# RWKV stage of a streaming-encoder layer: small products padded with zeros to the whole TensorE array

## The chip, the cores and the metric

One of the eight NeuronCores of a Trainium2 chip runs the whole kernel. A core has TensorE (PE: products of a stationary operand, loaded first, with a moving one), VectorE (DVE), ScalarE (ACT), GpSimd (POOL) and SyncE (SP, which issues the transfers here). The metric is the device time of one execution in microseconds (us).

## The reference

One layer mixes 4,096 tokens of width 1,024 in four head groups of width 256 and adds a gated embedding, a residual and a layer norm. The change touches the RWKV-7 group only: four heads of width 64, each with a 64x64 state that is updated token by token.

```python
def step(state, inp):
    w_t, r_t, k_t, v_t, kk_t, ab_t = inp
    sa = jnp.einsum('bhvk,bhk->bhv', state, -kk_t)
    state = (state * w_t[:, :, None, :] + sa[..., None] * ab_t[:, :, None, :]
             + v_t[..., None] * k_t[:, :, None, :])
    return state, jnp.einsum('bhvk,bhk->bhv', state, r_t)
```

The inputs of the step (receptance r, key k, value v, the decay w from a low-rank product, the removal key kk, the rate a) come from one projection of the tokens with a shift by one token. Behind the recurrence stand a norm by heads, a bonus term and a gate.

## The kernel before

The kernel runs pooling, retention, mLSTM, RWKV and the output stage one after another. The RWKV stage (`_rwkv_out`) takes the tokens in 16 blocks of 256, a block as four chunks of 64 (cc = 0, 1 picks a pair of chunks, e = 0, 1 the chunk in it), and solves the recurrence of a chunk in matrix form: products of decayed keys and queries (scores `gp`, kept in `g1`), the inverse `X` of a triangular 64x64 matrix per chunk and head (eight chunk pairs and heads side by side on the free axis), and a state `S` that is carried from chunk to chunk. The two chunks of a pair lie in the two halves of the 128 partitions; heads are counted by p and hh, with head hh in one half of the partitions where keys stand there.

All float32 products take two instructions each on TensorE; the dense projections (`la`, `k`, `r`, `v`, `g`) are exact splits into a high and a low part, three products each.

A block passes through pieces: the projections `la`, `k`, `r`, `v` and the gate `g`; `l` (low-rank decay and rate), `n` (norm of the removal key), `m` (elementwise keys and queries `BK`, `AR`), `bn` (bonus), `s0`, `s1` (transposed keys `ST`), `p0`, `p1` (scores), `vt` (transposed values into `SAV`), `inv` and `iv` (the diagonal blocks of 16 of the inverse: the matrix goes through DRAM to a layout with 64 partitions, 22 VectorE operations work on it, and the result goes through DRAM to X), and `pt`, `px`, `pu`, `py` (32x32 products that join the blocks of 16 to 32 and 64). `chain` runs the four chunks one after another, in three steps each:

- step 1: `ry` = AR S + (scores) SAV, and its half `bs` is copied to `R`;
- step 2: `sa` = X R, copied into the other half of `SAV`;
- step 3: `ds` = ST SAV updates the state (`Se` on POOL, four operations on VectorE, L657 to L661), and a last group of `ry` products gives the output.

The string ORDER sets how the pieces of three neighbouring blocks are woven together; TensorE keeps this order (`keep_in_program_order`). In iteration i the pieces marked .0 run for block i, those marked .1 for block i - 1, and each C is one step of the chain of block i - 2. "v.0/2" means two of the eight contraction steps of v; a dense step of two column halves is six products. Each iteration begins with

```python
C la.0 C k.0/2 C k.0 C r.0/2 C l.0 r.0/3 C r.0/2 n.0 r.0/2 C vt.1 r.0 m.0 C g.0/4 ...
```

so the first C (step 1 of chunk 0) and `la` stand ahead of the second C (step 2, `sa`), and `inv`, `iv` of block i are the last pieces of iteration i. The order on the other engines and the semaphores are made by a scheduler, from the accesses to tiles and their parts and from priorities (`soon()` raises one).

Of the kernel before, what the change touches and what calls it, by code (L numbers as in the profile page):

```python
# [29 lines left out]
ORDER = "C la.0 C k.0/2 C k.0 C r.0/2 C l.0 r.0/3 C r.0/2 n.0 r.0/2 C vt.1 r.0 m.0 C g.0/4 C g.0 v.0/2 C s0.0 v.0/1 pt.1 C p0.0/1 v.0/1 px.1 C p0.0 v.0/2 bn.0 v.0 pu.1 s1.0 p1.0/1 py.1 p1.0 inv.0 iv.0"  # L30
# [12 lines left out]
class Trunk:  # L43
# [27 lines left out]
    def fetch(self, hi, lo, src, nm, eng):  # L71
        """load float32 data and split it exactly into hi + lo"""
# [14 lines left out]
    def weights(self, name, g0, w=G, pool=None, bufs=5, gates=False):  # L87
        """hi and lo parts of columns g0..g0+w of a weight matrix"""
# [4 lines left out]
        lo = pool.tile([P, KT, c], F32R, name=f"wl_{name}_{g0}", tag=f"wl{tag}", bufs=bufs)  # L93
        hi = pool.tile([P, KT, c], F32R, name=f"wh_{name}_{g0}", tag=f"wh{tag}", bufs=bufs)
# [54 lines left out]
    def dense_k(self, jobs):  # L149
        """the same in steps of one contraction tile, in this order on the engine"""  # L150
# [19 lines left out]
    def silu_gate(self, sg, z):  # L170
        """twice z * sigmoid(z)"""
# [13 lines left out]
    # ------------------------------------------------------------------ RWKV  # L185
# [6 lines left out]
    def _rwkv_out(self, es):  # L192
# [17 lines left out]
        wla = self.lazy("w_rw", 3 * G, P)  # L210
# [3 lines left out]
        lraw = p1.tile([P, 2, P], F32, name="lraw", tag="km")  # L214
# [29 lines left out]
        zero = p1.tile([P, 512], F32, name="rzero", tag="km")  # L244
        Q.memset(zero, 0.0)
        for i in range(2):
# [3 lines left out]
            for e in range(2):  # L250
                nc.sync.dma_start(out=XD[i][:, e].rearrange("j a c -> j (a c)"), in_=zero[0:64])
        state = {"n": 0}
# [4 lines left out]
        def mixed(b, out, z, c0, n):  # L257
            """z + (previous token's z - z) * mu, by columns"""
# [11 lines left out]
        # what a block goes through, in pieces: generators that yield the time of the products they have issued  # L270
# [53 lines left out]
        def l(b):  # L324
            # low-rank decay and rate
# [4 lines left out]
            for g in range(2):  # L330
# [8 lines left out]
            tw = p1.tile([P, 2, TB], F32, name=f"tw{b}", tag="tw")  # L339
# [18 lines left out]
        def n(b):  # L358
            # squared norm of the removal key, by tokens in the order of the rows of its products
            k = bl[b]["k"]  # L360
            sq = p1.tile([P, 2, TB], F32, name=f"sq{b}", tag="km")
# [3 lines left out]
            for cc in range(2):  # L365
                for e in range(2):
                    for p in range(2):
                        t0 = cc * P + 64 * e
                        mm(n2[64 * (1 - e):64 * (1 - e) + 64, cc, 2 * p:2 * p + 2], sq[:, p, t0:t0 + 64], ones2,
                           start=True, stop=True)  # L370
            # rows (kappa, beta) of an even chunk, (beta, kappa) of an odd one
# [4 lines left out]
            for e in range(2):  # L376
                sl = slice(64 * (1 - e), 64 * (1 - e) + 64)
                Q.tensor_copy(out=rc[sl, :, e], in_=ri[sl])
# [8 lines left out]
        def m(b):  # L387
            k, r, ta, E, Ei = (bl[b][x] for x in ("k", "r", "ta", "E", "Ei"))
            km = p1.tile([P, 2, TB], F32, name=f"km{b}", tag="km")
# [5 lines left out]
            BK = p1.tile([P, 2, 2, 4, 64], F32, name=f"BK{b}", tag="BK")  # L395
# [14 lines left out]
            rk = p1.tile([P, 2, TB], F32, name=f"rk{b}", tag="tw")  # L410
            Q.tensor_tensor(out=rk, in0=r, in1=km, op=ALU.mult)
            ST = [p4.tile([P, 2, 2, P], F32, name=f"ST{b}_{cc}", tag="ST") for cc in range(2)]
            g1 = [p4.tile([P, 2, 2, 2, P], F32, name=f"g1{b}_{cc}", tag="g1") for cc in range(2)]
# [5 lines left out]
        def bn(b):  # L419
            rk = bl[b]["rk"]  # L420
            bn = wk.tile([P, 2, 4], F32, name=f"bn{b}", tag="wk")
            for cc in range(2):
                for e in range(2):
                    for p in range(2):
                        t0 = cc * P + 64 * e
                        mm(bn[64 * e:64 * e + 64, cc, 2 * p:2 * p + 2], rk[:, p, t0:t0 + 64], rkw[:, p],
                           start=True, stop=True)
# [5 lines left out]
        def s_(b, cc):  # L433
            # token-major copies of (kappa, beta)
# [11 lines left out]
        def p_(b, cc):  # L446
            # scores of the chunk
            BK, rc, AR, g1 = (bl[b][x] for x in ("BK", "rc", "AR", "g1"))
            gp = [wk.tile([P, 2, 2, P], F32, name=f"gp{b}_{cc}_{hh}", tag="wk") for hh in range(2)]
            for hh in range(2):  # L450
                sl = slice(64 * hh, 64 * hh + 64)
                for p in range(2):
                    for e in range(2):
                        mm(gp[hh][:, p, e], BK[sl, p, cc, 2 * e:2 * e + 2].rearrange("p a t -> p (a t)"),
                           AR[cc][sl, p, 2 * e:2 * e + 2].rearrange("p a t -> p (a t)"), start=True, stop=True)
                for p in range(2):
                    for e in range(2):
                        i = 2 * p + hh
                        V.scalar_tensor_tensor(out=g1[cc][:, hh, p, e], in0=gp[hh][:, p, e],  # L459
                                               scalar=rc[:, cc, e, i:i + 1], in1=msk[:, 64 * e:64 * e + P],  # L460
                                               op0=ALU.mult, op1=ALU.mult)
                yield 0.87
# [10 lines left out]
        def vt(b):  # L473
            v = bl[b]["v"]
            SAV = [p4.tile([P, 2, G], F32, name=f"SAV{b}_{cc}", tag="SAV") for cc in range(2)]
# [48 lines left out]
        def iv(b):  # L524
# [3 lines left out]
            with self.soon():  # L528
                # the four blocks of 4 on the diagonal, row by row from below
# [7 lines left out]
                # pairs of blocks: X12 = X11 (N12 X22), the inner product where N has zeros  # L537
# [17 lines left out]
                X = p2.tile([P, 8, 64], F32, name=f"X{b}", tag="X")  # L555
# [1130 lines left out]
```

## Time and profile before

| what | value |
|---|---|
| three runs | 2904.56, 2904.88, 2898.69 us, median 2904.56 |
| span of the profiled execution | 2898.2 us |
| TensorE busy | 2773.1 us |
| VectorE, GpSimd, ScalarE busy | 2270.0, 1156.9, 974.5 us |

The profile is that of one execution; its span runs from the first to the last instruction. What lies around the span is not shown for it; the fastest run shown is 0.5 us above the span, the median 6.4. The RWKV stage's products run from about 1,250 to 2,160 us. A row of the timeline shows the start in us from the span's start, the duration, the engine, the line of kernel.py, what is written and read, and the shapes; "x8" is a run of eight like instructions, whose duration is that from the first's start to the last's end. Since products are pipelined, the cost of one is the distance between starts, not its own duration. All small products are recorded under line 273, the helper `mm`; the tile's name tells them apart. "64*64" is the part of the array that the stationary operand fills, rows * columns. PEclk is the granted clock of TensorE: 1.0 is 2.4 GHz, 0.5 is 1.2 GHz.

### The profile page before, as it was taken

The numbers are of one execution on the slowest core, as the hardware profiler recorded it, in microseconds if no ns is written. First come the engines' busy times: TensorE is split into PE (matmuls) and PEld (weight loads), VectorE is DVE, ScalarE is ACT, GpSimd is POOL, SyncE is SP. The second block draws the span as 40 slices with busy tenths as digits, with TensorE's granted clock in tenths as the row PEclk, the third lists the DMA queues.
The fourth block names the chain that finished last, engine by engine and source line by source line (L and its number), as shares of the span: only waits on it lengthen the run. The fifth ranks groups of instructions, "written<-read, shape, count | busy, mean of one in ns | idle before, by whom it ended". The sixth has DMA issues, their size and how long they took to land.

```text
span 2898.2 us, 57364 instructions
## 1 busy us (share of the span) xinstructions
PE 2773.1 (96%) x21940; PEld 2466.1 (85%) x21940; DVE 2270.0 (78%) x5639; ACT 974.5 (34%) x2100; POOL 1156.9 (40%) x1231
## 2 busy tenths in 40 slices
PE   7899999999999999798999999999999999999997
PEld 7898888878999999688999999998998788777885
DVE  5657788887999999976777777778847566689997
ACT  3423223234433333333333333334423233432221
POOL 6654555553333333421232333223326111156665
PEclk9899999999999999888999999999999999999998
DMA  7743222223211111321111111112437444643441
GB/s 241 218 142 102 59 66 66 63 72 110 71 59 56 59 53 55 103 59 29 47 34 41 44 37 45 34 45 60 133 106 260 149 139 138 221 153 139 148 157 66
DMA packets 250499, 281.13 MB, mean 97 GB/s; under 512 B 69488, under 2 KB 166512, under 8 KB 250224
## 3 DMA queue, kind: packets, MB, share of 16 engines
q1 hardware_dynamic: 250224, 277.46, 30.5%
q8 instruction: 172, 2.82, 0.4%
q14 instruction: 103, 0.84, 0.1%
HBM read 209.69 MB, written 67.70 MB: 96 GB/s over the span
## 4 chain that ended last, share of the span: by engine, by line
PE 41%; DVE 10%; POOL 3%; DMA 2%; issue 2%; ACT 1%; SPq 0%; POOLq 0%; DVEq 0%; ACTq 0%
PE ry L273 3%; PE gp L273 2%; DVE ro L1578 2%; DVE ro L1557 1%; PE sa L273 1%; PE l L273 1%; PE zg L154 1%; DVE ro L1560 1%; PE zpl L147 1%; PE zpl L145 1%; PE zpl L146 1%; PE zg L155 1%; PE zg L156 1%; POOL ro L1561 1%; PE zpe L145 1%
## 5 line engine op out<-in xcount | busy, mean ns | idle before, releaser
L1336 ACT CAST Ah<-xr 128x512 fp32r<-128x512 f32 x189 | 117.0, 620 | 277.7 <-PE zrb L1372 58.7
L1337 DVE TENSOR_TENSOR Al<-xr,Ah 128x512 fp32r<-128x512 f32 x135 | 99.8, 739 | 76.5 <-ACT Ah L1336 75.7
L677 POOL TENSOR_TENSOR SAV<-SAV,bon 64x256 f32<-64x256 f32 x64 | 40.7, 636 | 283.9 <-PE ry L273 282.3
L85 DVE TENSOR_TENSOR xl<-rawx,xh 128x512 fp32r<-128x512 f32 x148 | 120.9, 821 | 39.8 <-ACT xh L84 38.9
L145 PE MATMUL zqk<-xh,wh_w_ml 128*128 128x256 f32 x512 | 149.1, 291 | 1.1 <-ACT xh L1078 1.1
L146 PE MATMUL zqk<-xl,wh_w_ml 128*128 128x256 f32 x512 | 149.1, 291 | 0.3 <-DVE xl L1079 0.3
L147 PE MATMUL zqk<-xh,wl_w_ml 128*128 128x256 f32 x512 | 149.2, 291 | 0.0
L84 ACT CAST xh<-rawx 128x512 fp32r<-128x512 f32 x148 | 91.6, 619 | 168.8 <-DMA rawx<-in_xT 72.3
L1337 POOL TENSOR_TENSOR Al<-xr,Ah 128x512 fp32r<-128x512 f32 x54 | 71.8, 1330 | 135.7 <-ACT Ah L1336 72.2
L1561 POOL TENSOR_TENSOR ro<-ro,ln_b 128x512 f32<-128x512 f32 x64 | 100.6, 1591 | 53.9 <-DVE ro L1560 53.9
L660 DVE SCALAR_TENSOR_TENSOR S<-ds,eC,Se 64x64 f32<-64x64 f32 x256 | 72.5, 283 | 53.4 <-PE ds L273 48.7
L866 POOL TENSOR_TENSOR rot<-rot,sw 128x256 f32<-128x256 f32 x64 | 69.4, 1085 | 94.2 <-DVE sw L865 88.5
L145 PEld LDWEIGHTS zqk<-xh,wh_w_ml 128*128 128x128 f32 x512 | 98.0, 191 | 3.6 <-ACT xh L1078 1.6
L147 PEld LDWEIGHTS zqk<-xh,wl_w_ml 128*128 128x128 f32 x512 | 98.1, 192 | 2.4
L146 PEld LDWEIGHTS zqk<-xl,wh_w_ml 128*128 128x128 f32 x512 | 98.2, 192 | 2.0 <-DVE xl L1079 0.8
L459 DVE SCALAR_TENSOR_TENSOR g<-gp,rc,c_rmask 128x128 f32<-128x128 f32 x256 | 72.1, 343 | 33.9 <-PE gp L273 32.8
L145 PE MATMUL zu<-xh,wh_w_pl 128*128 128x256 f32 x256 | 78.7, 308 | 14.7 <-ACT xh L84 8.9
L1356 POOL TENSOR_TENSOR xr<-xr,xr 128x512 f32<-128x512 f32 x27 | 35.5, 1316 | 141.8 <-DVE xr L1353 141.7
L146 PE MATMUL zu<-xl,wh_w_pl 128*128 128x256 f32 x256 | 78.2, 305 | 12.0 <-DVE xl L85 12.0
L1185 DVE SCALAR_TENSOR_TENSOR xc<-zc,c_convw,xc 128x256 f32<-128x256 f32 x192 | 86.2, 497 | 0.4
L273 PE MATMUL ry<-SAV,g 64*64 64x64 f32 (+1 forms) x1024 | 83.5, 223 | 0.0
L798 DVE SCALAR_TENSOR_TENSOR dp<-s,c_pinv,us 64x256 f32<-64x256 f32 (+1 forms) x64 | 44.5, 695 | 47.9 <-POOL s L784 41.7
(1120 smaller groups left out, 10675.9 us busy)
## 6 DMA issues: line engine op xcount, KB each, us to landing
rawx<-in_xT SPq DMA_DIRECT2D x148, 256.0 KB, 3.3
xr<-in_xT SPq DMA_DIRECT2D x108, 256.0 KB, 2.9
mr<-in_xT SPq DMA_DIRECT2D x64, 256.0 KB, 3.1
rp<-in_x SPq DMA_DIRECT2D x64, 256.0 KB, 3.1
s<-rp SPq DMA_DIRECT2D x64, 256.0 KB, 2.5
yo<-y SPq DMA_DIRECT2D x16, 1024.0 KB, 4.9
ro<-s SPq DMA_DIRECT2D x16, 1024.0 KB, 5.0
out<-ro SPq DMA_DIRECT2D x32, 512.0 KB, 2.6
```

The source lines that it names most:

```text
L84: nc.scalar.copy(out=hi, in_=raw)
L85: eng.tensor_tensor(out=lo, in0=raw, in1=hi.bitcast(F32), op=ALU.subtract)
L145: nc.tensor.matmul(out, lh(k), rh(k), start=(k == 0 and (apart or i == 0)), stop=False, skip_group_check=True)
L146: nc.tensor.matmul(out, lh(k), rl(k), start=False, stop=False, skip_group_check=True)
L147: nc.tensor.matmul(out, ll(k), rh(k), start=False, stop=(k == nk - 1), skip_group_check=True)
L273: mm = lambda *args, **kw: keep(nc.tensor.matmul(*args, **kw))
L459: V.scalar_tensor_tensor(out=g1[cc][:, hh, p, e], in0=gp[hh][:, p, e], scalar=rc[:, cc, e, i:i + 1], in1=msk[:, 64 * e:64 * e + P], op0=AL ...
L660: V.scalar_tensor_tensor(out=Sn[hv, p, hv], in0=ds[hv, p], scalar=eC[hv, p, c:c + 1], in1=Se[hv, p], op0=ALU.mult, op1=ALU.add)
L1185: V.scalar_tensor_tensor(out=xc[:, t], in0=zc[t // 2][:, t % 2, j:j + TB], scalar=cw[:, t, j:j + 1], in1=xc[:, t], op0=ALU.mult, op1=ALU.add)
L1336: self.nc.scalar.copy(out=hi, in_=src)
L1337: eng.tensor_tensor(out=lo, in0=src, in1=hi.bitcast(F32), op=ALU.subtract)
L1561: Q.tensor_tensor(out=rg, in0=rg, in1=ln["ln_b", g], op=ALU.add)
```

## The change

- The products of `ry`, `sa`, `l`, `n` and `bn` take all 128 rows and columns of the array. The operands that were cut to a half are replaced by tiles that hold zeros in the other half (`LZ`, `SAVS`, `G1` with three groups of 64 of which the middle one is zero, `RR`), cleared once at the start, `SAV` in each block. `n` and `bn` use half as many products. Output rows that hold nothing of use are not read.
- The inverses of two blocks live in one tile `XX` with 18 positions of 64 columns, and `sa` takes two neighbouring positions, of which one is the chunk's own.
- `ds` is two products of 128 columns in place of four of 64. The state update is one VectorE addition `T` = ds + S and four ScalarE scalings by the chunk's decay; `Se` on POOL is gone.
- The score products alternate between the two heads hh; all of a pair of chunks are one piece.
- ORDER changes from the second step of chunk 2 on: `bn` stands behind `g`, `p0` and `p1` are whole, `s1` and the last `v` steps stand between the chain's last step and `pu`, and `p1` comes ahead of `py`.
- Room for it: BK, tw and km move to a weight buffer that `la`'s narrower weights leave free; `lraw`, the zeros for DRAM and a tile of the gated embedding use another tag.

```diff
-ORDER = "... C g.0/4 C g.0 v.0/2 C s0.0 v.0/1 pt.1 C p0.0/1 v.0/1 px.1 C p0.0 v.0/2 bn.0 v.0 pu.1 s1.0 p1.0/1 py.1 p1.0 inv.0 iv.0"
+ORDER = "... C g.0/4 C g.0 bn.0 v.0/2 C s0.0 v.0/1 pt.1 C p0.0 v.0/2 px.1 C v.0/1 s1.0 v.0/2 pu.1 v.0/1 p1.0 v.0 py.1 inv.0 iv.0"
...
+        LZ = [cp.tile([P, 2, P], F32R, name=f"LZ{g}", tag=f"LZ{g}") for g in range(2)]
...
+            Q.memset(LZ[g][other].bitcast(F32), 0.0)
+            A.copy(out=LZ[g][own], in_=lraw[own])
...
+        SAVS = [[cp.tile([P, 2, G], F32, ...) for cc in range(2)] for i in range(2)]
+        own_ = self.wp.tile([P, 2 * D], F32, name="own", tag="wlg")
+        BK_ = own_[:, 0:D].rearrange("p (a c g t) -> p a c g t", a=2, c=2, g=4)
+        tw_, km_ = (own_[:, o:o + H].rearrange("p (a t) -> p a t", a=2) for o in (D, D + H))
+        G1 = [[cp.tile([P, 2, 2, 2, 3, 64], F32, ...) for cc in range(2)] for i in range(2)]
+        XX = cp.tile([P, 18, 64], F32, name="XX", tag="XX")
+        RR = [cp.tile([P, 2, P], F32, name=f"RR{e}", tag=f"RR{e}") for e in range(2)]
+        for t in [t for x in SAVS + G1 for t in x] + RR + [XX]:
+            Q.memset(t, 0.0)
...
+            for g in range(2):
                 for p in range(2):
                     mm(lz[g][:, p], LW[g][:, p], lah[:, g], start=(p == 0), stop=False, skip_group_check=True)
-                    mm(lz[g][:, p], LW[g][own, p], lal[own], start=False, stop=True, skip_group_check=True)
+                for p in range(2):
+                    mm(lz[g][:, p], LZ[g][:, p], lal, start=False, stop=(p == 1), skip_group_check=True)
...
-                for e in range(2):
-                    for p in range(2):
-                        t0 = cc * P + 64 * e
-                        mm(n2[64 * (1 - e):64 * (1 - e) + 64, cc, 2 * p:2 * p + 2], sq[:, p, t0:t0 + 64], ones2, ...)
+                for p in range(2):
+                    mm(n2[:, cc, 2 * p:2 * p + 2], sq[:, p, cc * P:cc * P + P], ones2, start=True, stop=True)
...
-            for hh in range(2):
-                sl = slice(64 * hh, 64 * hh + 64)
-                for p in range(2):
-                    for e in range(2):
+            for p in range(2):
+                for e in range(2):
+                    for hh in range(2):
+                        sl = slice(64 * hh, 64 * hh + 64)
                         mm(gp[hh][:, p, e], BK[sl, p, cc, 2 * e:2 * e + 2]..., AR[cc][sl, p, 2 * e:2 * e + 2]..., ...)
...
+                    Q.memset(SAV[cc][64 * (1 - e):64 * (1 - e) + 64, e], 0.0)
...
-                X = p2.tile([P, 8, 64], F32, name=f"X{b}", tag="X")
+                X = XX[:, 8 * (b % 2) + 1:8 * (b % 2) + 9]
...
                     for p, hh, hv in heads:
-                        mm(ry[bs, p, hv], g1[cc][ks, hh, p, e, bs],
-                           SAV[cc][ks, e, P * p + 64 * hh:P * p + 64 * hh + 64], ...)
-                    R = p1.tile([P, 2, P], F32, name=f"R{b}_{c}", tag="R")
+                        mm(ry[:, p, hv], g1[cc][:, hh, p, e].rearrange("p g t -> p (g t)")[:, 64 * (1 - e):64 * (1 - e) + P],
+                           SAV[cc][:, e, P * p + 64 * hh:P * p + 64 * hh + 64], ...)
                     A.copy(out=R[bs], in_=ry[bs])
...
                     for p, hh, hv in heads:
-                        mm(sa[bs, p, hv], X[bs, 4 * cc + 2 * hh + p], R[bs, p, hv], start=True, stop=True)
+                        i = 8 * (b % 2) + 4 * cc + 2 * hh + p + e
+                        mm(sa[:, p, hv], XX[:, i:i + 2].rearrange("p a c -> p (a c)"), R[:, p, hv], start=True, stop=True)
...
-                        mm(ds[hv, p], ST[cc][:, e, p, hv], SAV[cc][:, e, P * p + 64 * hh:P * p + 64 * hh + 64], ...)
-                    Se = p1.tile([P, 2, 64], F32, name=f"Se{b}_{c}", tag="Se")
-                    ...  Q.tensor_tensor(out=Se[hv], in0=S_[hv, :, hv], in1=eC..., op=ALU.mult)
-                    ...  V.scalar_tensor_tensor(out=Sn[hv, p, hv], in0=ds[hv, p], scalar=eC[hv, p, c:c + 1], in1=Se[hv, p], ...)
+                    for p in range(2):
+                        mm(ds[:, p], ST[cc][:, e, p], SAV[cc][:, e, P * p:P * p + P], start=True, stop=True)
...
-                        mm(ry[ks, p, hv], g1[cc][:, hh, p, e, ks],
+                        mm(ry[:, p, hv], g1[cc][:, hh, p, e].rearrange("p g t -> p (g t)")[:, 64 * e:64 * e + P],
                            SAV[cc][:, e, P * p + 64 * hh:P * p + 64 * hh + 64], ...)
+                    T = p1.tile([P, 2, P], F32, name=f"T{b}_{c}", tag="T")
+                    V.tensor_tensor(out=T, in0=ds, in1=S_, op=ALU.add)
+                    for p, hh, hv in heads:
+                        A.mul(out=Sn[hv, p, hv], in_=T[hv, p, hv], mul=eC[hv, p, c:c + 1])
```

Lines that only lose a comment, and renames that follow from the above, are left out.

## Rows read from the trace of the kernel before

**Rows 1.** the page: engine totals (part 1) and one costly group (part 5)

```profile
PE 2773.1 (96%) x21940; PEld 2466.1 (85%) x21940; DVE 2270.0 (78%) x5639; ACT 974.5 (34%) x2100; POOL 1156.9 (40%) x1231
...
L660 DVE SCALAR_TENSOR_TENSOR S<-ds,eC,Se 64x64 f32<-64x64 f32 x256 | 72.5, 283 | 53.4 <-PE ds L273 48.7
```

**Rows 2.** two windows: stretch, length, busy time by engine (count), PEclk, DMA share, GB/s

```profile
1324.00:1336.00 12.00, 11.98 (x183) 10.99 (x184) 5.40 (x15) 1.67 (x4) 0.00 (x0) 0.54 0.12 34
1614.00:1624.00 10.00, 10.00 (x86) 9.07 (x86) 6.96 (x25) 3.73 (x10) 2.19 (x5) 0.83 0.02 4
```

**Rows 3.** timeline of PE in one block of the stage: start us, duration us, instruction, count

```profile
1601.21 0.28 PE L155 MATMUL zla<-xl,wh_w_rw 128*128 128x256 f32 x1
1601.33 0.28 PE L156 MATMUL zla<-xh,wl_w_rw 128*128 128x256 f32 x1
1601.54 0.68 PE L273 MATMUL sa<-R,X 64*64 64x64 f32 x8
...
1602.36 0.28 PE L155 MATMUL z7k<-xl,wh_w_rw 128*128 128x256 f32 x1
...
1603.77 0.45 PE L273 MATMUL ds<-SAV,ST 128*64 128x64 f32 x8
1604.05 0.63 PE L273 MATMUL ry<-SAV,g 128*64 128x64 f32 x8
...
1604.83 0.28 PE L155 MATMUL z7k<-xl,wh_w_rw 128*128 128x256 f32 x1
...
1609.03 0.61 PE L273 MATMUL ry<-S,AR 128*128 128x128 f32 x4
1609.57 0.67 PE L273 MATMUL ry<-SAV,g 64*64 64x64 f32 x8
...
1610.39 0.28 PE L155 MATMUL z7r<-xl,wh_w_rw 128*128 128x256 f32 x1
...
1612.40 0.38 PE L273 MATMUL l<-lah,LW 128*128 128x256 f32 x1
...
1614.90 0.48 PE L154 MATMUL z7r<-xh,wh_w_rw 128*128 128x256 f32 x1
...
1636.98 1.16 PE L273 MATMUL gp<-AR,BK 64*128 64x128 f32 x8
...
1643.18 0.65 PE L273 MATMUL bn<-rkw,rk 128*64 128x2 f32 x16
```

**Rows 4.** timeline of PE in the retention stage

```profile
504.91 0.71 PE L920 MATMUL sc<-qT,kT 64*128 64x128 f32 x8
...
510.24 1.00 PE L930 MATMUL yy<-vh,Pm 128*128 128x64 f32 x8
...
511.36 0.39 PE L1373 MATMUL zrc<-rB3whg,Al 128*128 128x512 f32 x1
...
511.59 0.40 PE L1371 MATMUL zrd<-rB,Ah 128*128 128x512 f32 x1
```

**Rows 5.** timeline of VectorE, from one block's last score to its inverse's use

```profile
1598.97 1.13 DVE L459 SCALAR_TENSOR_TENSOR g<-gp,rc,c_rmask 128x128 f32<-128x128 f32 x4
...
1607.16 0.16 DVE L527 TENSOR_TENSOR nt<-nt,xs 64x4 f32<-64x4 f32 x1 [0.22 <-DMA nt<-nd]
...
1611.76 0.59 DVE L527 TENSOR_TENSOR nt<-nt,xs 64x256 f32<-64x256 f32 x1
...
1612.83 0.59 DVE L527 TENSOR_TENSOR nt<-nt,xs 64x256 f32<-64x256 f32 x1
...
1622.50 0.39 DVE L552 TENSOR_REDUCE xs<-nt 64x32 f32<-64x256 f32 x1
...
1629.83 0.71 DVE L567 STREAM_TRANSPOSE Z<-X 128x512 f32<-128x512 f32 x1
```

**Rows 6.** timeline of PE, the wait for the first inverse at the stage's start

```profile
1324.02 1.05 PE L273 MATMUL pt<-Z,g 32*32 32x16 f32 x64 [7.32 <-DVE Z L567]
```

**Rows 7.** groups of POOL by line at the stage's start: one memset

```profile
L245 POOL MEMSET rzero<- 128x512 f32 x1 | 0.5, 537 | 0.0
```

More of the change, by code (lines that the diff above doesn't have):

```diff
@@ L85, in fetch, with weights @@
         eng.tensor_tensor(out=lo, in0=raw, in1=hi.bitcast(F32), op=ALU.subtract)
-    def weights(self, name, g0, w=G, pool=None, bufs=5, gates=False):
+    def weights(self, name, g0, w=G, pool=None, bufs=5, gates=False, one=False):
         nc = self.nc
@@ L92, in weights @@
         c = G + 8 if gates else G
-        lo = pool.tile([P, KT, c], F32R, name=f"wl_{name}_{g0}", tag=f"wl{tag}", bufs=bufs)
-        hi = pool.tile([P, KT, c], F32R, name=f"wh_{name}_{g0}", tag=f"wh{tag}", bufs=bufs)
+        if one:
+            t = pool.tile([P, 2, KT, w], F32R, name=f"w_{name}_{g0}", tag=f"wh{tag}", bufs=bufs)
+            hi, lo = t[:, 0], t[:, 1]
+        else:
+            lo = pool.tile([P, KT, c], F32R, name=f"wl_{name}_{g0}", tag=f"wl{tag}", bufs=bufs)
+            hi = pool.tile([P, KT, c], F32R, name=f"wh_{name}_{g0}", tag=f"wh{tag}", bufs=bufs)
         def parts():
@@ L209, in _rwkv_out @@
         wg = [self.lazy("w_rw", i * G) for i in range(3)]
-        wla = self.lazy("w_rw", 3 * G, P)
+        wla = self.lazy("w_rw", 3 * G, P, one=True)
         wgate = self.lazy("w_rw", 3 * G + P)
         prm, omu = self.prm, self.omu
-        lraw = p1.tile([P, 2, P], F32, name="lraw", tag="km")
+        lraw = p1.tile([P, 2, P], F32, name="lraw", tag="v")
         nc.sync.dma_start(out=lraw, in_=a["lora"].rearrange("r (p c) -> r p c", p=2))
         LW = [cp.tile([P, 2, P], F32R, name=f"LW{g}", tag=f"LW{g}") for g in range(2)]
+        LZ = [cp.tile([P, 2, P], F32R, name=f"LZ{g}", tag=f"LZ{g}") for g in range(2)]
         for g in range(2):
@@ L243, in _rwkv_out @@
         Q.memset(TD, 0.0)
-        zero = p1.tile([P, 512], F32, name="rzero", tag="km")
+        zero = p1.tile([P, 512], F32, name="rzero", tag="v")
         Q.memset(zero, 0.0)
@@ L251, in _rwkv_out @@
                 nc.sync.dma_start(out=XD[i][:, e].rearrange("j a c -> j (a c)"), in_=zero[0:64])
+        SAVS = [[cp.tile([P, 2, G], F32, name=f"SAV{i}{cc}", tag=f"SAV{i}{cc}") for cc in range(2)] for i in range(2)]
+        own_ = self.wp.tile([P, 2 * D], F32, name="own", tag="wlg")
+        BK_ = own_[:, 0:D].rearrange("p (a c g t) -> p a c g t", a=2, c=2, g=4)
+        tw_, km_ = (own_[:, o:o + H].rearrange("p (a t) -> p a t", a=2) for o in (D, D + H))
+        G1 = [[cp.tile([P, 2, 2, 2, 3, 64], F32, name=f"G1{i}{cc}", tag=f"G1{i}{cc}") for cc in range(2)] for i in range(2)]
+        half2 = lambda t: t.rearrange("p (a t) -> p a t", t=64)
+        XX = cp.tile([P, 18, 64], F32, name="XX", tag="XX")
+        RR = [cp.tile([P, 2, P], F32, name=f"RR{e}", tag=f"RR{e}") for e in range(2)]
+        for t in [t for x in SAVS + G1 for t in x] + RR + [XX]:
+            Q.memset(t, 0.0)
         state = {"n": 0}
@@ L360, in n @@
             k = bl[b]["k"]
-            sq = p1.tile([P, 2, TB], F32, name=f"sq{b}", tag="km")
+            sq = km_
             for p in range(2):
@@ L376, in n @@
             for e in range(2):
-                sl = slice(64 * (1 - e), 64 * (1 - e) + 64)
-                Q.tensor_copy(out=rc[sl, :, e], in_=ri[sl])
+                Q.tensor_copy(out=rc[64 * (1 - e):64 * (1 - e) + 64, :, e], in_=ri[64 * e:64 * e + 64])
             bl[b]["rc"] = rc
@@ L388, in m @@
             k, r, ta, E, Ei = (bl[b][x] for x in ("k", "r", "ta", "E", "Ei"))
-            km = p1.tile([P, 2, TB], F32, name=f"km{b}", tag="km")
+            km = km_
             for p in range(2):
@@ L394, in m @@
             V.tensor_scalar(out=ta, in0=ta, scalar1=-0.5, scalar2=-0.5, op0=ALU.mult, op1=ALU.add)
-            BK = p1.tile([P, 2, 2, 4, 64], F32, name=f"BK{b}", tag="BK")
+            BK = BK_
             AR = [p4.tile([P, 2, 4, 64], F32, name=f"AR{b}_{cc}", tag="AR") for cc in range(2)]
@@ L409, in m @@
                                 op=ALU.mult)
-            rk = p1.tile([P, 2, TB], F32, name=f"rk{b}", tag="tw")
+            rk = tw_
             Q.tensor_tensor(out=rk, in0=r, in1=km, op=ALU.mult)
             ST = [p4.tile([P, 2, 2, P], F32, name=f"ST{b}_{cc}", tag="ST") for cc in range(2)]
-            g1 = [p4.tile([P, 2, 2, 2, P], F32, name=f"g1{b}_{cc}", tag="g1") for cc in range(2)]
+            g1 = G1[b % 2]
             bl[b].update(rk=rk, BK=BK, AR=AR, ST=ST, g1=g1)
@@ L474, in vt @@
             v = bl[b]["v"]
-            SAV = [p4.tile([P, 2, G], F32, name=f"SAV{b}_{cc}", tag="SAV") for cc in range(2)]
+            SAV = SAVS[b % 2]
             t = wk.tile([P, 2, 2, P], F32, name=f"vt{b}", tag="wk")
@@ L630, in chain @@
                 heads = [(p, hh, slice(64 * hh, 64 * hh + 64)) for p in range(2) for hh in range(2)]
+                R = RR[e]
                 with self.soon():
@@ L649, in chain @@
                 with self.soon():
-                    ds = ch.tile([P, 2, 64], F32, name=f"ds{b}_{c}", tag=DS)
+                    ds = ch.tile([P, 2, P], F32, name=f"ds{b}_{c}", tag=DS)
+                    for p in range(2):
+                        mm(ds[:, p], ST[cc][:, e, p], SAV[cc][:, e, P * p:P * p + P], start=True, stop=True)
                     for p, hh, hv in heads:
-                        mm(ds[hv, p], ST[cc][:, e, p, hv], SAV[cc][:, e, P * p + 64 * hh:P * p + 64 * hh + 64],
-                           start=True, stop=True)
-                    Se = p1.tile([P, 2, 64], F32, name=f"Se{b}_{c}", tag="Se")
-                    for hh in range(2):
-                        hv = slice(64 * hh, 64 * hh + 64)
-                        Q.tensor_tensor(out=Se[hv], in0=S_[hv, :, hv],
-                                        in1=eC[hv, :, c:c + 1].broadcast_to([64, 2, 64]), op=ALU.mult)
-                    for p, hh, hv in heads:
-                        V.scalar_tensor_tensor(out=Sn[hv, p, hv], in0=ds[hv, p], scalar=eC[hv, p, c:c + 1],
-                                               in1=Se[hv, p], op0=ALU.mult, op1=ALU.add)
-                    for p, hh, hv in heads:
-                        mm(ry[ks, p, hv], g1[cc][:, hh, p, e, ks],
+                        mm(ry[:, p, hv], g1[cc][:, hh, p, e].rearrange("p g t -> p (g t)")[:, 64 * e:64 * e + P],
                            SAV[cc][:, e, P * p + 64 * hh:P * p + 64 * hh + 64],
                            start=False, stop=(p == 1 and hh == 1), skip_group_check=True)
+                    T = p1.tile([P, 2, P], F32, name=f"T{b}_{c}", tag="T")
+                    V.tensor_tensor(out=T, in0=ds, in1=S_, op=ALU.add)
+                    for p, hh, hv in heads:
+                        A.mul(out=Sn[hv, p, hv], in_=T[hv, p, hv], mul=eC[hv, p, c:c + 1])
                     A.copy(out=Y[ks, cc], in_=ry[ks].rearrange("p a v -> p (a v)"))
```

34 lines of the change are left out of this document (15 added, 19 removed).

## The prediction

> **What bounds the kernel now.** I read the page first, then the windows, then the timelines of TensorE and VectorE. The page's totals show TensorE busy for 96% of the span and VectorE for 78% [rows 1]. Cut into windows, TensorE reads fully busy in every block of the RWKV stage, 1,340 to 2,160 us (one such window stands in [rows 2]). So the stage costs what its products cost in their written order. It loses time in two ways: a change between array shapes, and a granted clock that drops.
>
> The timeline shows the first [rows 3]. Dense products start 0.12 us apart (1601.21, 1601.33); the first 64x64 product follows after 0.21, and on the way back the second dense start is late as well. The lora products alternate between 128 and 64 rows and take 1614.90 - 1612.40 = 2.50 us for eight, 0.31 each. Behind them the granted clock falls to its lower level, 1.2 GHz, for a part of the next products: it reads 0.83 over ten microseconds [rows 2]. Six of the fourteen windows that I read at this place show it.
>
> Last I followed the inverse. A block's last score copy ends at 1598.97 + 1.13 = 1600.10, and the first user of its inverse X starts at 1629.83 [rows 5]. Nothing waits for that now: the pair products stand late in the next block.
>
> **The wider products.** The price of a full-width product with 64 columns is in the retention stage: eight of yy, between 512-column products 0.23 apart, cost 511.36 - 510.24 - 0.23 = 0.89 us, 0.111 each [rows 4]. The score products there alternate heads too.
>
> Per chunk [rows 3]:
> - sa: 1602.36 - 1601.33 - 2 x 0.12 = 0.79 now, then 8 x 0.111 = 0.89: +0.10.
> - first ry group: 1610.39 - 1609.03 - 0.12 = 1.24, then 12 x 0.111 = 1.33: +0.09.
> - ds and second ry: 1604.83 - 1603.77 - 0.12 + 0.09 (its late start) = 1.03. Two ds products of 128 columns are four instructions in place of eight, so 12 x 0.111 = 1.33: +0.30.
>
> That is +0.49, over 64 chunks +31 us. Per block, times 16:
> - lora: 2.50 to 8 x 0.12 = 0.96: -25 us.
> - scores: a group of eight spans 1.16 now [rows 3] and 0.71 with heads alternating [rows 4]: -0.45, four groups: -29 us.
> - n and bn: 0.65 now, 8 x 0.111 = 0.89 then, less two shape changes of 0.09: +0.06 each, +2 us.
> - the 32x32 products of the inverse and the scores now stand between full-width ones, and no longer share a shape change with a small neighbour: some six changes of 0.1 per block, +10 us.
> - the drops of the clock behind lora: 0.83 over 10 us loses at most 1.7, say 1.5; in 6 of 14 blocks, so 7 of 16: -10 us.
>
> Sum for TensorE: -21 us. Bounds: -41 if the padding (+31) and the shared changes (+10) cost half of that; +8 if the scores gain nothing.
>
> The Trainium skill (TensorEngine Tiling (Array Packing), Key Properties) says that tiles of the array work independently and that a change of tiling mode drains the engine. The 0.21 us agrees with the second. By the first alone, padding would be a pure loss: at the spacing inside a group, 0.065 to 0.111 for sa and so on, about 1.4 us per chunk and +89 us where the rows above give +31.
>
> **The shared X tile.** The inverses of two blocks now lie side by side in XX: positions 1 to 8 for even blocks, 9 to 16 for odd ones. sa loads a window of two positions that starts at 8(b%2) + 4cc + 2hh + p + e. For an odd block's first product all but b%2 are zero: the window is positions 8 and 9, and 8 is the last inverse of the next, even block. Its values meet zero rows of R and fall on output rows that nobody reads, but it is a read of what a DMA writes. The chain runs two blocks behind; in iteration i it handles i - 2, and X of i - 1 was begun at the end of iteration i - 1. So in every odd iteration the second step of the chain must wait for an inverse that now lands late in the iteration. This sa is at 1601.54 in [rows 3], while that X is first used at 1629.83 [rows 5]: 28.3 us. The last position of an even block also reaches over (8 and 9 at e = 1), but in chunk 3, after pt has already needed that X.
>
> TensorE keeps program order, so everything stands behind that sa: the rest of the chain, k, r, lora, scores. ScalarE and VectorE then run dry for want of products. On SP nothing new is put ahead of the inverse's transfers.
>
> Length of the wait, from the last score copy:
> - through DRAM to the first step of the inverse: 1607.16 - 1600.10 = 7.1 us.
> - the VectorE steps: 4.6 us to the first large pair (1611.76), with work for k in between, and four pairs of 1.07 (1612.83 - 1611.76): 8.9. With the k work stuck behind the waiting product, about 8.0.
> - back through DRAM to use: 1629.83 - 1622.89 = 6.9.
>
> Together 22.0. sa comes 1601.54 - 1600.10 = 1.4 after that copy now; in the new order py stands between the last scores and the next block, and all eight score copies of the pair queue on VectorE at once. I take 2.4 (bounds 1.4 and 3.4). The wait is 19.6 us.
>
> After it the clock is at its lower level for a while. At the stage's start, where pt waited 7.3 us for the first X [rows 6], it read 0.54 over the next 12 us [rows 2], a loss of at most 5.5 us. Small shapes ran there; here more dense ones follow. Between 1.5 (the drop behind lora) and 5.5 I take 2.5. The wait occurs for chain blocks 1, 3, ... 13 (block 15 has no successor): 7 x 22.1 = +155 us. Bounds: 7 x (16.8 + 1.5) = +128, with the VectorE steps at an estimated 6.2 us and a gap of 3.4; and 7 x 28.3 = +198 if nothing of the chain shortens.
>
> **The rest, costed at nothing.** The state update: four VectorE operations of 0.283 [rows 1] become one add (at most 0.59, by the 64x256 row in [rows 5]) and four ScalarE scalings, estimated at the same 0.283. The state is ready about 0.8 us later. This is covered by the dense steps between chunks (behind the first chunk 36 products of 0.12, 4.3 us); with the cover gone it would be 64 x 0.8 = 51 us. ScalarE gains some 72 us of work at 34% busy [rows 1]. Y's copy is queued behind the scalings, and the next user of ry is behind the same dense steps. POOL loses the 128 Se products and gains 64 small memsets, and at the start about 10,000 elements per partition of zeroing, by 537 ns for 512 [rows 7] about 10 us. The products of the first block cover it; if not, +10 us. The reordered bn, s1 and v only move inside a busy TensorE.
>
> **Sum.** +155 - 21 = +134 us on the profiled span of 2898.2, so 3032; the runs shown lie 0.5 to 6.7 above that span, their median 6.4. I say 3035.
>
> **Rivals.**
> - The wait doesn't bite: dependencies are ordered so that sa runs ahead, or X lands earlier than the rows say. Then only TensorE's -21 us is left: about 2880, faster. It decides at a wait of 21 / 7 = 3 us per odd block. For it: the values read are never used. Against it: 22 us of chain against 2.4 us of lead.
> - The wait comes in every block, if XX is tracked as one object: 15 x 22.1 - 21 = +310, 3211. For it: the pools release a tile as one object (reuse_waits="tile" in the code). Against it: that speaks of a buffer's reuse, and XX is never reused.
> - No wait, and padding eats the gains (scores gain nothing, +8): about 2909, slower by a little.
>
> **Chances.** The wait in odd blocks 0.82, no wait 0.11, every block 0.04, padding alone 0.03. Changes under 0.2%, about 6 us, can't be told from none. Faster 0.10, same 0.02, slower 0.88. The range is the first case with its bounds: +87 (128 - 41) gives 2988, with a margin 2970; +206 (198 + 8) gives 3107, so 3105. It leaves out about 2 in 10.
>
> **What will show it.** Right: in odd iterations only, the chain's sa is idle some 20 us with X's transfer, or the step before it, as releaser, TensorE at 0.5 for a few us after; eight sa products 0.11 apart and no late start before them; lora at 0.12 with no drop of the clock; scores under 0.07 apart. Wrong: even spacing of the blocks near 50 us means that no wait exists; waits in both parities mean the second rival; a late state shows as waits of ry for S.

## The result, and the profile after

The changed kernel takes 3053.36 us (median of four runs, 3050.18 to 3056.76) against 2904.42 for the kernel before in the same comparison: a ratio of 1.0523 [1.0508, 1.0537]. It is slower by about 150 us, where 3035 was forecast. The profiled execution spans 3054.0 us, 155.8 more than before.

The page's totals of the kernel after, with one costly group and the three longest waits of TensorE (us in total, times, longest):

```profile
PE 2783.1 (91%) x21428; PEld 2526.6 (83%) x21428; DVE 2238.9 (73%) x5447; ACT 1061.2 (35%) x2358; POOL 1104.4 (36%) x1180
...
L293 PE MATMUL sa<-RR,XX 128*128 128x64 f32 x512 | 74.3, 292 | 136.4 <-DMA XX<-xd 135.2
```

```profile
PE sa L293 <- DMA XX<-xd: 135.2, 7, 19.6
PE scm L1225 <- DVE xc L1205: 12.7, 3, 10.1
PE zu L150 <- DVE xl L85: 11.2, 9, 4.0
```

TensorE's busy time hardly moves (2773.1 in [rows 1]); its share falls from 96% to 91%. One wait has appeared: `sa` on a transfer that writes XX, seven times, 19.3 us in the mean. In the timeline it stands in every second block. Below are the first `la` products of three neighbouring blocks, 50.2 and 72.4 us apart; the long one holds the `sa` that sat idle for 19.24 us:

```profile
1587.05 0.36 PE L158 MATMUL zla<-xh,w_w_rw 128*128 128x256 f32 x1
...
1637.22 0.36 PE L158 MATMUL zla<-xh,w_w_rw 128*128 128x256 f32 x1
...
1640.05 0.28 PE L160 MATMUL zla<-xh,w_w_rw 128*128 128x256 f32 x1
1659.57 1.94 PE L293 MATMUL sa<-RR,XX 128*128 128x64 f32 x8 [19.24 <-DMA XX<-xd]
1663.98 1.05 PE L293 MATMUL ds<-SAV,ST 128*128 128x128 f32 x4
...
1709.62 0.36 PE L158 MATMUL zla<-xh,w_w_rw 128*128 128x256 f32 x1
```

What `sa` waits for is the inverse of the next, even block. VectorE and SyncE's queue in the same stretch:

```profile
1636.91 2.15 DVE L475 SCALAR_TENSOR_TENSOR G<-gp,rc,c_rmask 128x128 f32<-128x128 f32 x8
...
1644.72 0.15 DVE L544 TENSOR_TENSOR nt<-nt,xs 64x4 f32<-64x4 f32 x1
...
1652.35 0.41 DVE L569 TENSOR_REDUCE xs<-nt 64x32 f32<-64x256 f32 x1
1652.79 1.78 SPq L571 DMA_DIRECT2D xd<-xs  x4
1655.96 1.13 SPq L574 DMA_DIRECT2D XX<-xd  x2
1659.56 0.71 DVE L584 STREAM_TRANSPOSE Z<-XX 128x512 f32<-128x512 f32 x1 [6.79 <-DMA XX<-xd]
```

The last score copy ends at 1639.06. From there it is 5.7 us to the first step of the inverse, 8.0 of steps and 6.8 back through DRAM, and `sa` and the transpose of `pt`, the first true user, start together. TensorE stands still meanwhile, ScalarE and GpSimd run dry within 5 us, and VectorE does little but the inverse's steps. Behind the wait the granted clock is low for a few us (windows: stretch, length, busy by engine, granted clock, DMA share, GB/s):

```profile
1644.00:1648.00 4.00, 0.00 (x0) 0.00 (x0) 3.65 (x14) 0.30 (x1) 0.52 (x1) 0.63 0.20 67
...
1660.00:1664.00 4.00, 4.00 (x21) 4.00 (x21) 0.27 (x1) 0.37 (x1) 0.00 (x0) 0.50 0.00 0
1664.00:1668.00 4.00, 4.00 (x30) 4.00 (x30) 0.42 (x1) 1.75 (x5) 0.92 (x2) 0.81 0.00 0
```

From 1659.57 to 1664 at half speed and 4 us at 0.81: 2.2 + 0.8 = 3.0 us lost. From 1668 on it reads 1.00 again.

What the widening itself did to the products shows in the same block, later:

```profile
1672.90 0.28 PE L159 MATMUL z7r<-xl,wh_w_rw 128*128 128x256 f32 x1
1673.02 0.28 PE L160 MATMUL z7r<-xh,wl_w_rw 128*128 128x256 f32 x1
1673.14 1.00 PE L293 MATMUL sa<-RR,XX 128*128 128x64 f32 x8
1673.95 0.48 PE L293 MATMUL l<-lah,LW 128*128 128x256 f32 x2
1674.27 0.40 PE L293 MATMUL l<-lal,LZ 128*128 128x256 f32 x2
...
1674.99 0.28 PE L158 MATMUL z7r<-xh,wh_w_rw 128*128 128x256 f32 x1
...
1698.06 1.16 PE L293 MATMUL gp<-AR,own 64*128 64x128 f32 x16
```

Eight `l` products take 1674.99 - 1673.95 = 1.04 us, where eight took 2.50 [rows 3]. Sixteen score products fit into the 1.16 us of eight. `sa` costs 1673.95 - 1673.02 - 0.12 = 0.81 to the next product; narrow, by the same reckoning, it is 0.69 (the median over the stage before).

### The profile page after: what moved, and what is told of

It reads as the page before. It is cut to its first block, busy times and chain, and to the rows that moved or that the text cites. A ratio compares the mean times of both kernels' runs of the same rounds, so it can differ in the third digit from the quotient of the medians.

```text
span 3054.0 us, 56285 instructions
## 1 busy us (share of the span) xinstructions
PE 2783.1 (91%) x21428; PEld 2526.6 (83%) x21428; DVE 2238.9 (73%) x5447; ACT 1061.2 (35%) x2358; POOL 1104.4 (36%) x1180
## 4 chain that ended last, share of the span: by engine, by line
PE 30%; DVE 15%; DMA 6%; POOL 4%; issue 3%; ACT 2%; SPq 1%; POOLq 0%; DVEq 0%; ACTq 0%
PE ry L293 4%; PE sa L293 2%; DVE ro L1593 2%; DVE G L475 2%; DVE ro L1572 1%; DVE ro L1575 1%; DVE nt L544 1%; POOL ro L1576 1%; PE zg L158 1%; DVE so L1567 1%; DMA nd<-G 1%; PE zg L159 1%; PE zg L160 1%; ACT S L680 1%; PE ds L293 1%
## 5 line engine op out<-in xcount | busy, mean ns | idle before, releaser
L293 PE MATMUL sa<-RR,XX 128*128 128x64 f32 x512 | 74.3, 292 | 136.4 <-DMA XX<-xd 135.2
L293 PEld LDWEIGHTS sa<-RR,XX 128*128 128x128 f32 x512 | 67.9, 206 | 142.6 <-issue 137.1
L293 PE MATMUL ry<-SAV,G 128*128 128x64 f32 x1024 | 130.5, 271 | 0.0
L293 PEld LDWEIGHTS ry<-SAV,G 128*128 128x128 f32 x1024 | 127.3, 195 | 0.0
L680 ACT ACTIVATE S<-T,eC 64x64 f32<-64x64 f32 x256 | 88.4, 345 | 89.8 <-DVE T L678 85.1
L475 DVE SCALAR_TENSOR_TENSOR G<-gp,rc,c_rmask 128x128 f32<-128x128 f32 x256 | 69.2, 343 | 39.7 <-PE gp L293 39.7
```

Source lines behind the costliest of these rows:

```text
L293: mm = lambda *args, **kw: keep(nc.tensor.matmul(*args, **kw))
L475: V.scalar_tensor_tensor(out=g1[cc][:, hh, p, e, 0::2], in0=half2(gp[hh][:, p, e]), scalar=rc[:, cc, e, i:i + 1], in1=half2(msk[:, 64 * e: ...
L680: A.mul(out=Sn[hv, p, hv], in_=T[hv, p, hv], mul=eC[hv, p, c:c + 1])
```

## The experiments

A period below is the distance in the timeline between the first `la` products of two neighbouring blocks, the tail the rest of the span behind block 15's. Before, the periods from the third on are 50.67 us, or some 52.15 in five of these thirteen, where the clock drops behind `l`, and the tail is 889.9.

**Without the shared position.** Odd blocks move up by one, so the position between two blocks belongs to neither.

```diff
-        XX = cp.tile([P, 18, 64], F32, name="XX", tag="XX")
+        XX = cp.tile([P, 19, 64], F32, name="XX", tag="XX")
-                X = XX[:, 8 * (b % 2) + 1:8 * (b % 2) + 9]
+                X = XX[:, 9 * (b % 2) + 1:9 * (b % 2) + 9]
-                        i = 8 * (b % 2) + 4 * cc + 2 * hh + p + e
+                        i = 9 * (b % 2) + 4 * cc + 2 * hh + p + e
```

> The changed kernel with one unused position between the inverses of even and odd blocks (19 positions, odd blocks from 9), so that sa of an odd block no longer touches the neighbour's inverse. Theory, the neighbour's position is what sa waits for: no wait of sa for a transfer, all blocks near 50.3 us, and the seven times 22.1 us gone: about 2898 us. Rival 1, the shared tile is tracked as one object: the waits stay or move, about 3050. Rival 2, a good part of the loss is padding or the clock: still over 2920.

Measured: 2912.60 us, ratio to the kernel before 1.0037 [1.0023, 1.0051]. The wait on the transfer is gone and the long periods with it; from the third on they average 51.0 us. In the stage, TensorE's waits now begin with

```profile
PE sa L293 <- ACT RR L657: 7.4, 7, 2.4
PE zpl L149 <- ACT ep L1453: 5.7, 3, 3.4
```

The shared position thus costs 3053.4 - 2912.6 = 141 us. But what is left is 11 us slower than before, not 21 faster, and the tail is 911.9, 22 longer. The next runs ask why.

**The same, with the embedding's tile elsewhere.** `ep` shares a buffer with `v` in the changed kernel; here it takes the tag "ta".

> The same with the first blocks' result of the gated embedding in the buffer of ta in place of that of v. Theory, the 13.7 us lost behind the fifteenth block come from that shared buffer, which is busy with v until the last vt: about 2885 us, with the embedding's products starting some 42 us into the sixteenth iteration as before. Rival, they come from the weight buffer that BK, tw and km now hold, or from the longer ScalarE queue: no change against the run with the gap alone, about 2898.

Measured: 2918.47, ratio 1.0059 [1.0046, 1.0072], tail 911.3. The buffer is not the cause of the long tail, and its theory fails.

**The low-rank products alone.** The kernel before with the `LZ` lines of the diff and its `l` loop (and `ep` in "ta").

> The kernel before with the lora products alone on all 128 rows (a zero-padded copy of the low-rank weights; the gated embedding's first results use the buffer of ta to make room). Theory, the 2.50 us for eight are shape changes and the drop of the clock follows from them: lora 0.96 us, no drop behind it, 16 x 1.54 + 10 = 35 us less, about 2869. Rival, the drop comes from elsewhere in the block: 25 us less, about 2879. Rival, another engine sets the pace once TensorE is faster: under 10 us less.

Measured: 2872.52, ratio 0.9900 [0.9886, 0.9914]. Every period from the third on is 49.13 now, 1.54 less than the undisturbed 50.67, and the granted clock reads 1.00 from 1,400 to 2,000 us. The tail stays at 888.4.

**The alternating scores alone,** in the kernel before with its old ORDER:

```diff
-            for hh in range(2):
-                for p in range(2):
-                    for e in range(2):
+            for p in range(2):
+                for e in range(2):
+                    for hh in range(2):
...
-                yield 0.87
+            yield 0.87
```

> The kernel before with the score products alone alternating between the heads (both heads of a chunk pair in one piece, at the place of the first). Theory, 0.45 us per group of eight and a shape change less per pair: 29 to 35 us less, about 2872. Rival, VectorE's eight score copies then come in one go and hold the next products: under 10 us less or slower.

Measured: 2936.61 (2903.96 to 2947.61), ratio 1.010 [1.0065, 1.0136]: slower, though the products run at twice the pace as they should. The profiled execution is the longest of the six; its periods are 54.6 us. Its timeline and windows of one block:

```profile
1827.23 0.48 PE L273 MATMUL gp<-AR,BK 64*128 64x128 f32 x2
1828.57 1.16 PE L273 MATMUL gp<-AR,BK 64*128 64x128 f32 x14 [0.86 <-DVE ST L440]
```

```profile
1825.00:1830.00 5.00, 3.90 (x80) 3.20 (x80) 4.97 (x17) 2.25 (x6) 2.98 (x4) 1.00 0.29 98
1830.00:1835.00 5.00, 5.00 (x47) 4.62 (x41) 4.20 (x13) 0.37 (x1) 1.40 (x2) 0.55 0.27 79
1835.00:1840.00 5.00, 5.00 (x40) 4.66 (x40) 1.71 (x6) 0.90 (x3) 1.51 (x3) 0.77 0.30 67
...
1850.00:1855.00 5.00, 5.00 (x29) 4.49 (x29) 1.70 (x3) 2.25 (x6) 0.38 (x1) 0.66 0.25 50
```

The scores of the second pair wait for the copy `ST` on VectorE, 0.9 us in 15 blocks, 12.4 us in all. That would not lose what the pace wins. But behind it the granted clock falls to its lower level, and again behind `l`: 5 x 0.45 + 5 x 0.23 + 5 x 0.34 = 5.1 us per block. The six executions differ in the same way: the shortest, 2903.96 us, has a mean granted clock of 0.973, the other five, 2932 us and more, 0.955 to 0.960. So my -29 held for the products and not for the kernel. Two theories were left: the order, which puts `s1`, `p1` side by side, or the clock behind `l`.

**All but the chain, and both halves of the question.** First the kernel before with wide `l`, `n` and `bn`, alternating scores and the new ORDER, but its own chain, state update and X; then wide `l` and alternating scores in the old ORDER.

> The kernel before with all of the change but the chain's products, the state update and the buffer X: wide low-rank products, wide n and bn, alternating scores, the new order of the stages. Theory A (what the kernel without the waits lost against my sum, some 30 us, comes from the chain: its padded products and its state update): the low-rank part measured alone gives -29, the alternating scores give my -29, together about 2845 us, block periods near 47.3 us (49.13 less 1.8) and a tail of 888 us as before. Rival B (the alternating scores cost what they save, as they did alone, where a wait of 0.9 us per block on the copy ST and a granted clock of 0.90 took the place of the gain): 2872 us or more, periods of 49 us or more, and a clock of 0.9 in the blocks.

> The kernel before with wide low-rank products and alternating scores, in the old order of the stages. Theory A (the loss of the scores alone lay in the order: nothing stands between the transposes of the second chunk pair and its scores, so they wait 0.9 us for ST and the clock falls behind them): the wait stays here and with it the clock, so about 2900 us, against 2845 in the new order. Rival B (the clock drops came from the low-rank products, which are mended here): 2845 us, periods near 47.3 us.

Measured: 2858.32, ratio 0.9856 [0.9843, 0.9869], and 2894.48, ratio 0.9978 [0.9967, 0.9990]. The order is worth some 36 us. (The first of the two also has wide `n` and `bn`; the run with narrow ones, below, differs from the second in ORDER alone and takes 2857.76.) The traces show the difference where `ST` is copied on VectorE. In the old order:

```profile
1845.38 0.16 DVE L728 TENSOR_SCALAR rsr<-mvr 128x8 f32<-128x8 f32 x1
1845.45 0.68 DVE L731 TENSOR_TENSOR Y<-Y,mvr 128x512 f32<-128x512 f32 x1
1846.05 0.68 DVE L445 TENSOR_TENSOR ST<-st,rc 128x512 f32<-128x512 f32 x1
```

and in the new:

```profile
1810.80 0.69 DVE L597 STREAM_TRANSPOSE Z<-X 128x512 f32<-128x512 f32 x1
1811.53 0.69 DVE L438 TENSOR_TENSOR ST<-st,rc 128x512 f32<-128x512 f32 x1
```

In the old order `ST` stands behind the head norm of the chain's output, and the scores behind `ST`; in the new one it follows the transpose at once. `pu` waits 0.6 us for that transpose in 12 blocks, and the clock reads 1.00 from 1,400 to 1,900 us; in the old order, where the scores wait up to 0.9 us for `ST` in all 16 blocks (13.1 us), the window behind those shown (1850 to 1855) reads 0.50. ORDER moves several pieces, and they were not tried one by one. Theory A of these two runs holds, except that the first is 13 us above its 2845. Its steady periods are 47.70, near the 47.3 expected; the tail is 896.7, 8 longer, and two waits of 4 us in the gated embedding behind the stage are new.

**The old scores and order in the widened kernel,** and **the old state update** there (GpSimd and four VectorE operations again, `ds` still wide), both with 19 positions in XX:

> The changed kernel with 19 positions in XX (no waits on the other block's transfers) and with the old score products and the old order of the stages. Theory A (alternating scores are worth their 1.8 us per block): 2912.6 + 29 = 2941 us. Rival B (scores and order are worth nothing in a kernel with the padded chain): 2912 us within 5, and the tail after the last block's first products stays near 912 us.

> The changed kernel with 19 positions in XX and with the old state update (product of state and decay on GpSimd beside the products, four scalar_tensor_tensor on VectorE behind them). Theory A (the state's way over VectorE and four scalings of 0.345 us on ScalarE is late where few other products stand between two chunks, in the last two blocks): the tail falls from 912 us towards 895, the time to about 2897 us. Rival B (the tail comes from the padded products alone): 2912 us within 5, tail unchanged.

Measured: 2946.68, ratio 1.0158 [1.0145, 1.0172], and 2923.72, ratio 1.0082 [1.0069, 1.0094]. Scores and order are worth 34 us here (2912.6 with them). The state update is no loss: going back costs 11 us, with `sa` waiting for `RR` 14.5 us in place of 7.4, and the tail (910.6) is as before. So the tail does not come from the state update, as theory A had it.

**Narrow `n` and `bn`, and one piece of `v` moved,** both on the kernel without the change of the chain; the second is the first with

```diff
-p0.0 v.0/2 px.1 C v.0/1 s1.0 v.0/2 pu.1
+p0.0 v.0/1 px.1 C v.0/1 s1.0 v.0/3 pu.1
```

> The kernel before with wide low-rank products, alternating scores and the new order of the stages; n and bn stay on half the array, the chain is that of before. By the traces n and bn cost 0.81 us each when wide and 0.67 when narrow, so 16 x 0.28 = 4.5 us less than the same kernel with wide n and bn (2858.3): 2854 us. If the reordered bn and not its width made the difference: 2858 us.

> The same with one piece of v moved from behind the scores of the first chunk pair to ahead of pu. pu waits 0.6 us in each block for Z on VectorE where scores alternate; with 0.7 us more work ahead of it this wait should go: 16 x 0.6 = 9 us, 2845 us. Rival: px, which now has one piece less between it and pt, waits instead, and the time stays at 2854 or rises by the clock behind the wait.

Measured: 2857.76, ratio 0.9849 [0.9836, 0.9861], no different from 2858.3: the steady period falls by 0.24 us where 0.28 was forecast, but the tail is 4.7 longer (901.4); and 2898.78, ratio 0.9987 [0.9973, 1.0001]. The move meant to save 9 us costs 41. The wait of `pu` did not go; it doubled, to 1.3 us in 12 blocks. VectorE, TensorE and the windows of one:

```profile
1887.08 0.69 DVE L445 TENSOR_TENSOR ST<-st,rc 128x512 f32<-128x512 f32 x1
1887.69 0.70 DVE L604 STREAM_TRANSPOSE Z<-X 128x512 f32<-128x512 f32 x1
```

```profile
1888.54 0.69 PE L276 MATMUL pu<-Z,g 32*32 32x32 f32 x32 [1.30 <-DVE mvr L726]
```

```profile
1885.00:1890.00 5.00, 3.70 (x65) 3.48 (x66) 4.86 (x18) 2.38 (x6) 1.00 (x3) 1.00 0.24 72
1890.00:1895.00 5.00, 5.00 (x58) 4.47 (x57) 4.92 (x17) 0.85 (x3) 2.02 (x1) 0.55 0.38 118
1895.00:1900.00 5.00, 5.00 (x36) 4.80 (x36) 1.77 (x4) 1.43 (x5) 0.00 (x0) 0.77 0.20 26
```

With `pu` later in the order, the copy `ST` is now ahead of the transpose `Z` on VectorE, and `pu` needs Z (the releaser named, mvr, is the work behind it on VectorE). Behind the wait the clock falls: 5 x 0.45 + 5 x 0.23 = 3.4 us. With the 0.7 of longer wait that is 4.1, where the periods differ by 3.6 (51.1 against 47.45). But the first three times this wait occurs, the clock does not fall behind it; windows of ten us behind the second and the fourth:

```profile
1429.00:1439.00 10.00, 10.00 (x136) 9.21 (x129) 7.16 (x21) 2.48 (x7) 4.47 (x5) 1.00 0.29 74
1531.00:1541.00 10.00, 10.00 (x96) 9.27 (x97) 7.45 (x22) 2.47 (x7) 4.63 (x5) 0.66 0.29 74
```

The two periods that hold the first two of these waits are 48.18 and 48.19, so the longer wait alone costs 0.7 and the clock behind it some 2.9.

**The narrow chain in the changed kernel.** Everything of the change, XX with 19 positions, but `ry`, `sa` and `ds` on parts of the array; for `sa`, for instance:

```diff
-                        mm(sa[:, p, hv], XX[:, i:i + 2].rearrange("p a c -> p (a c)"), R[:, p, hv],
+                        mm(sa[bs, p, hv], XX[bs, 9 * (b % 2) + 1 + 4 * cc + 2 * hh + p], R[bs, p, hv],
```

(`T` is then added in two halves, so that nothing unwritten of `ds` is read.)

> The changed kernel with 19 positions in XX and with the chain's products on tiles of the array again (ry and sa on 64x64, ds and the second ry on 128x64), but with the new state update, buffers and everything else of the change. Theory A (the padding of the chain's products and of their neighbours costs 3.1 us per block by the traces): 2912.6 less 50, about 2862 us, periods near 47.9 us. Rival B (the state update and the shared buffers carry a good part of the 54 us that separate it from the kernel without the change of the chain): above 2885 us.

Measured: 2859.62, ratio 0.9862 [0.9847, 0.9876]. Theory A holds: padding the chain costs 2912.6 - 2859.6 = 53 us, and the state update, the zeroed tiles and the weight buffer together next to nothing (2858.3 without them). One group of each, wide and narrow, between dense products:

```profile
1801.45 0.28 PE L160 MATMUL z11k<-xh,wl_w_rw 128*128 128x256 f32 x1
1801.57 0.61 PE L293 MATMUL ds<-SAV,ST 128*128 128x128 f32 x4
1802.02 1.00 PE L293 MATMUL ry<-SAV,G 128*128 128x64 f32 x8
1802.83 0.36 PE L158 MATMUL z11k<-xh,wh_w_rw 128*128 128x256 f32 x1
1803.04 0.28 PE L159 MATMUL z11k<-xl,wh_w_rw 128*128 128x256 f32 x1
```

```profile
1820.46 0.28 PE L160 MATMUL z12k<-xh,wl_w_rw 128*128 128x256 f32 x1
1820.67 0.45 PE L293 MATMUL ds<-SAV,ST 128*64 128x64 f32 x8
1820.95 0.63 PE L293 MATMUL ry<-SAV,G 128*64 128x64 f32 x8
1821.51 0.39 PE L158 MATMUL z12k<-xh,wh_w_rw 128*128 128x256 f32 x1
```

Less one dense step of 0.12, that is 1.26 us wide and 0.93 narrow.

## Why the prediction was right, and where a term was off

**The wait: right in place, mechanism and size.** It occurs seven times, in odd iterations only, and the run with the spare position shows the reason given. By its parts, on the block shown: 5.7 + 8.0 + 6.8 from the last score copy to the use, less a lead of 1.3, where 7.1 + 8.0 + 6.9 less 2.4 stood: 19.2 against 19.6. That it comes so near is in part luck: the way to the first step was 1.4 too long and the lead 1.1. The clock behind it cost 3.0, not 2.5. The long periods stand 22.0 above the even ones, where 22.1 was forecast. The waits were worth 141 us in all and not 155. Six of them lie in the 15 periods, which are 126 us shorter without them, 21.0 each: the kernel's blocks then take 51.0 us, not the 50.3 of the changed kernel's even blocks, and `sa` waits for `RR` 7.4 us in all in place of 0.4. The seventh lies behind block 15's first products, and the tail falls by 13.8 only (925.7 to 911.9).

**The term that was mis-sized is TensorE's -21:** without the waits the kernel is +11 (2912.6 against 2901.5), 32 us off, and outside the +8 of my bounds. Three parts of it:

- *lora*, forecast -25 for the products and -10 for the clock: -29 measured. The products gave 50.67 - 49.13 = 1.54 per block, the forecast's 25 / 16. That leaves 4 of the 10 for the clock. The profile before has the drop behind `l` in five periods, 7.4 us in all, not in seven blocks; all five are gone, but the period with the wait for the first inverse takes 53.92 us where it took 52.17.
- *scores, n and bn*, forecast -27: from 2872.5 (lora alone) to 2859.6 (all but the padded chain) it is -13. In the steady blocks the forecast is exact: 49.13 - 47.45 = 1.68 per block, 27 over 16. The rest goes in the first blocks of the stage and in a tail that is 7 us longer (895.6 against 888.4). And the gain hung on the new order, which the prediction took for a mere shuffle "inside a busy TensorE": in the old order the alternating scores lose, 22 us beside the wide `l` (2894.5 against 2872.5).
- *padding of the chain*, forecast +31 and +10 for shape changes no longer shared: +53. The product prices were right: by the prediction's reckoning, to the second dense start, `sa` takes 0.09 more (forecast 0.10), the first `ry` 0.09 (0.09), `ds` and the second `ry` 0.31 (0.30), each a median over the lone groups of the stage. With the neighbours' changes the undisturbed periods differ by 2.76 (50.21 against 47.45), which is 44 us over 16 blocks where 41 were forecast. What the sum lacked are the other 9. The tail alone is 16 us longer than with the narrow chain (911.9 against 895.6), though the chains of only three blocks lie in it. It is not longer by waits: TensorE is idle for 52.2 us of it, 50.8 with the narrow chain. In its first 250 us the distances between starts of `sa`, `ry` and `ds` add up to 49.6 us against 33.2. Why they cost more there than in the blocks was not taken apart.

The two errors, +32 and -14, leave 3035 eighteen short of 3053. Their signs are opposite, so it is luck that the sum came nearer than TensorE's term alone did.

**What I costed at nothing.** Scaling on ScalarE takes 345 ns apiece, not 283 [rows 1], but no wait of weight comes from it: undoing it made things worse. GpSimd's clearing at the start is not seen: the first `la` products stand at 1249.17, against 1248.34 before.

**The rivals.** That no wait bites, and that it comes in every block, are both ruled out: it stands in the odd iterations alone. "Padding alone" (2909) is close to what the kernel does once the wait is taken out (2912.6), yet for other reasons: the scores did gain, and the padding cost more.

**The rule on tiles.** The Trainium skill (TensorEngine Tiling (Array Packing), Key Properties) says that a change of tiling mode drains the engine. The runs agree for `l`, as far as its price goes: products that alternate between 128 and 64 rows cost 0.31 us each, products of one shape 0.13 (1.04 for eight). They also show that it is not the whole price: behind the wide `ry` too the second dense product starts 0.21 after the first and not 0.12 (1802.83, then 1803.04 above), so widening does not buy that back. The Trainium skill lists in the same section that tiles work independently. For the chain, whose groups keep one shape, the runs go with that: by the medians a lone group of narrow `sa`, or of `ry`, is shorter than its full-width form (0.69 against 0.81, 1.15 against 1.26). That the independence is the reason is not shown.

## What to carry to other kernels

- Pad a product to the whole array where it alternates with another shape product by product (`l`: -29 us); leave it on its tiles where a whole group keeps one shape (the chain: +53 us). The version that does the first without the second is the fastest here, 2858 us, 1.5% below the kernel before.
- Padding reads what it does not need. Ask of each widened operand whose data the extra columns are and when they are written: one shared position of 64 columns cost 141 us, and one spare position took it away.
- A faster group of products changes who waits. Where TensorE has no slack, look at the granted clock behind each new wait: 1.3 us per block cost 0.7 more than the wait of 0.6 before where the clock held, and 3.6 more where it fell.

## What the runs showed of the hardware

- A short wait can cost several times its length, by the clock behind it, but need not. In the kernel with the moved piece the wait of 1.3 us at `pu` occurs twelve times: behind the first three the clock reads 1.00, behind the other nine it falls (0.66 over ten us from 1531). In the old order with wide `l` the wait of 0.9 us for `ST` is followed by 0.50 over the ten us from 1589.5, and by 1.00 over those from 1489 and 1541. Behind 0.6 us at `pu`, in the new order, it stays at 1.00. So the length of the wait alone does not decide; what does was not tested.
- Three kernels scatter more between executions than the rest: the alternating scores alone (2903.96 to 2947.61 us), the old order with wide `l` (2888.09 to 2907.53) and the moved piece (2883.27 to 2906.25), in 6, 12 and 12 executions; all others, the 17 of the kernel before among them, stay within 11 us. In these three the clock falls behind short waits, and the executions with the lower mean clock are the longer ones: with the moved piece, 0.969 at 2883.27 and 0.961 at 2906.25. Why it falls more often in one execution than in another is not shown.
- Score products with heads alternating, on the two 64-row halves of the array, run at just twice the pace: 16 in 1.16 us, against 8 in 1.16 us with one half after the other [rows 3].
